# A two-layer decoder trunk on one core: in layer 1's channel mixer the last plain chunk of columns moves to the front, and the last grouped one ends the mixer with its columns turned one token tile at a time

## The chip, the core and the metric

The kernel runs on one core of a Trainium2 chip. The engines that matter here are TensorE (PE in the profile; PEld is its weight load), VectorE (DVE), ScalarE (ACT), GpSimd (POOL) and SyncE (SP), which issues most DMA loads. Each engine works through its own queue in order and waits on semaphores for the others. The metric is the device time of one launch in microseconds (us), lower is better; before the change it is 571.77 us, the median of three runs (570.83 to 571.89).

## What is computed

256 tokens of width 1024 go through two layers. Each layer is a token mixer beside a small cross-attention, an output projection and a LayerNorm, and then the channel mixer, which is all that the change touches:

```python
def swiglu(x, w_in, w_out):
    g, u = jnp.split(x @ w_in, 2, axis=-1)
    return (jax.nn.silu(g) * u) @ w_out

x = layer_norm(ALPHA * x + swiglu(x, w_ffn_in[i], w_ffn_out[i]), ln_ffn_g[i], ln_ffn_b[i])
```

`w_in` is 1024 x 5632 and `w_out` 2816 x 1024, all in float32.

## The kernel before

**Split numbers.** Every matmul operand is written as a high and a low part: ACT rounds a value to the multiplier's format (`split`, L234) and DVE subtracts that from the original (L235). A product takes three matmuls (high x high, high x low, low x high). So each weight passes over ACT and over DVE before TensorE can use it. `Stream` does this in *halves*: a 1 MB unit of weights is loaded into one of four raw buffers and split in two halves of 128 x 1024 into one of ten split buffers (`HALF_BUFS`). The order of the halves is that of `ffn_steps`, so the table in that function sets the loads, the splits and the matmuls alike. TensorE's order is that of the code; the other engines' order is set by a scheduler at build time.

**Chunks.** The 2816 columns are eleven chunks of 256. A *plain* chunk ("R", `chunk_in`) multiplies the 256 tokens (two token tiles of 128, written tt 0 and 1) by the chunk's gate and value columns in four steps (i = 0 to 3) of one half each. A *grouped* pair of chunks ("S", `product`) gets by with seven products instead of eight, by sums of quarters (in Strassen's way): M1, M5, M2, M3, M6, M7, M4, two halves each. The left sums are made once a layer (`sums`, tiles `Sg`). The weight sums are made by DVE on the raw operands: an add of 128 x 2048 (L189) ahead of M5, M6 and M4; for M7 a load that accumulates does it (L192). Operands "11" and "21" have one buffer each for all groups (tags `gb` and `vbig`); `gb` also takes the final LayerNorm's scale and shift (`gb1ffn`). PSUM tiles X, Y and Z take the products. After some products DVE combines them: m1 += Y (L605), u2 += Z (L609), m1 = -m1*u2 (L610), m5 += X (L612, after M7 and before M4 overwrites X), m5 = -m5*silu (L616).

**Out.** A chunk's activations are turned by four transposes (`transposes`, L625; tile `tp`, split into `htg`), and `chunk_out` multiplies them by two halves of `w_out` ("out" steps, `spl_w`) into the accumulators `fog`. Each "out" step for both token tiles is twelve matmuls of 128 x 512, as long as one product or one step of a plain chunk.

**Order of layer 1 before.** R0 and R1 (with tile 0's steps first, since tile 1's input comes later), then S2, S4, S6, S8, then R10. The out steps of earlier chunks stand between the products. At the end `end_tile(0)` finishes tile 0 with chunks 9 and 10 and its LayerNorm starts; `last_tile(1)` runs chunks 8 to 10 of tile 1 in three column pieces, each followed by its part of the last LayerNorm, and the results are stored.

Of the kernel before, what the change touches and what calls it, by code (L numbers as in the profile page):

```python
# [21 lines left out]
P = 128  # L22
# [13 lines left out]
NFF = D_FF // 256  # L36
# [3 lines left out]

PLAN = (("R", 0), ("R", 1), ("S", 2), ("S", 4), ("S", 6), ("S", 8), ("R", 10))
PRODUCTS = ("M1", "M5", "M2", "M3", "M6", "M7", "M4")

OPERAND = {"M1": ("11", None), "M5": ("11", "12"), "M2": ("21", None), "M3": ("22", None),
# [4 lines left out]
def ffn_steps(l):  # L51

    steps, due, prev = [], [], []
    for kind, c in PLAN:
        new = [("out", p, k, (0, 1)) for p in prev for k in range(2)]
        if kind == "S":


            ins = [("s", c, m) for m in PRODUCTS]
            due += new  # L60
            early, due = due[:-3], due[-3:]
            steps += [ins[0], ("tp",), *early[:1], ins[1], *early[1:], *ins[2:5], due[0], ins[5], due[1], ins[6]]
            due = due[2:]
        else:
            ins = [("r", c, i, (0, 1)) for i in range(4)]
            if l == 1 and c == 0:

                steps += [*(("r", 0, i, (0,)) for i in range(4)), *(("r", 1, i, (0,)) for i in range(2)), ("x",)]
            elif l == 1 and c == 1:
                steps += [*(("r", 1, i, (0,)) for i in range(2, 4)), *(("r", 0, i, (1,)) for i in range(4)),  # L70
                          *(("r", 1, i, (1,)) for i in range(2)), ("tp",), *(("r", 1, i, (1,)) for i in range(2, 4))]
                due = new
            elif c == NFF - 1:
                steps += [ins[0], ("tp",), *due, *ins[1:], *(("out", NFF - 3, k, (0,)) for k in range(2)), ("tp",)]
            elif c:
                steps += [ins[0], ("tp",), *ins[1:]]
                due = new
            else:
                steps += ins
        prev = [c, c + 1] if kind == "S" else [c]  # L80
    return steps
# [140 lines left out]
def build(nc, tc, ins, out):  # L222
    ET = mybir.EngineType
    with (
# [44 lines left out]
        for i in range(WARM):  # L269
            nc.tensor.matmul(wt[:, :P], warm, warm, start=True, stop=True)  # L270
        ident = const.tile([P, P], F32, name="ident")
# [6 lines left out]
            out=maskb, in_=maskb, compare_op=ALU.is_ge, fill=NEG, base=0,  # L278
# [248 lines left out]
        class Ffn:  # L527
# [52 lines left out]
            def product(self, c, m):  # L580


                if m == "M1":
                    self.X, self.Y, self.Z = (mm_tile(f"{n}{self.nm}{c}") for n in "XYZ")
                dst = {"M1": self.X, "M6": self.X, "M7": self.X, "M4": self.X, "M2": self.Y}.get(m, self.Z)
                alone = m in ("M1", "M5", "M2")
                for x in range(2):
                    w = stream.get(f"s{self.l}_{c}", m, x)
                    for k in range(2):
                        for n, (a, b) in enumerate(PASSES):  # L590
                            mm(dst, self.left[m](a, 2 * x + k), w[:, b, k * 512:(k + 1) * 512],
                               alone and x == 0 and k == 0 and n == 0, x == 1 and k == 1 and n == 2, not alone)
                    stream.done(f"s{self.l}_{c}", m, x)

                def kept(n, src):
                    t = work_tile(f"{n}{self.nm}{c}")
                    nc.scalar.copy(t, src)
                    return t

                if m == "M1":  # L600
                    self.m1 = kept("m1", self.X)
                elif m == "M5":
                    self.m5 = kept("m5", self.Z)
                elif m == "M2":
                    nc.vector.tensor_add(self.m1, self.m1, self.Y)  # L605
                    nc.scalar.activation(self.m1, self.m1, AF.Silu)
                elif m == "M6":
                    u2 = kept("u2", self.X)
                    nc.vector.tensor_add(u2, u2, self.Z)  # L609
                    nc.vector.scalar_tensor_tensor(self.m1, self.m1, -1.0, u2, ALU.mult, ALU.mult)  # L610
                elif m == "M7":
                    nc.vector.tensor_add(self.m5, self.m5, self.X)  # L612
                elif m == "M4":
                    sg = work_tile(f"sg{self.nm}{c}")
                    nc.scalar.activation(sg, self.X, AF.Silu)
                    nc.vector.scalar_tensor_tensor(self.m5, self.m5, -1.0, sg, ALU.mult, ALU.mult)  # L616
                    self.pending.append([(c + j, [h[:, 256 * j:256 * j + 256] for h in (self.m1, self.m5)])
                                         for j in range(2)])

            def transposes(self):  # L620

# [13 lines left out]
            def run(self, mid=None):  # L635
                for st in ffn_steps(self.l):
                    self.tp_tiles()
                    if st[0] == "r":
                        self.chunk_in(*st[1:])
                        if st[1:3] == (NFF - 1, 0):  # L640
                            stream.held = {"gb", "vbig"}
                            self.gb = load_gb(self.l, "ffn")
                    elif st[0] == "s":
                        self.product(*st[1:])
                    elif st[0] == "x":
                        mid()
                    elif st[0] == "tp":
                        if self.pending:
                            self.transposes()
                    else:  # L650
                        self.chunk_out(*st[1:])
                return self.gb
# [57 lines left out]
        for i in range(4):  # L710
# [11 lines left out]
            out=wsT, in_=wsT, compare_op=ALU.is_ge, fill=0.0, base=0,  # L722
# [9 lines left out]
        for h in range(2):  # L732
            for tt in range(2):
                sl = slice(h * 384, (h + 1) * 384)
# [9 lines left out]
        for j in range(4):  # L744
            t = actp.tile([P, 2, 512], F32R, tag="hm", name=f"memT{j}", bufs=4)
# [39 lines left out]
        gb = load_gb(0, "mix")  # L785
# [16 lines left out]
        ffn = Ffn(0, x_of(x1T), xres, "f")  # L802
        stream.held.clear()
        ffn.sums(A)
        gb = ffn.run()
# [72 lines left out]
        for i in range(6):  # L878
# [16 lines left out]
            if i == 2:  # L895
                gb = load_gb(1, "mix")
# [29 lines left out]
            ffn.sums(A)  # L926

        gb = ffn.run(second_tile)
        ffn.end_tile(0).finish(gb, store=True)
        ffn.last_tile(1).finish(gb, store=True)  # L930


# [5 lines left out]
def _pack(inp):  # L938
    a, b = inp["a_w_in"][0], inp["b_w_in"][0]
    kv, wo, fi, fo = inp["w_mem_kv"], inp["w_mix_out"], inp["w_ffn_in"], inp["w_ffn_out"]  # L940
    blk = {}
    for i in range(4):
        blk[f"v{i}"] = _cols(a, 2 * i, 2 * i + 2, W_MIX, 2 * W_MIX)
        blk[f"bv{i}"] = _cols(b, 2 * i, 2 * i + 2, 2 * W_MIX, 3 * W_MIX)
    blk["qm0"] = _cols(a, 0, KT, 2 * W_MIX, 2 * W_MIX + W_MEM)
    blk["qm1"] = _cols(b, 0, KT, 3 * W_MIX, 3 * W_MIX + W_MEM)
    for i in range(3):
        blk[f"u{i}"] = _cols(a, 0, KT, 256 * i, 256 * i + 256)
    for l in range(2):
        blk[f"km{l}"] = _cols(kv[l], 0, KT, 0, W_MEM)  # L950
        blk[f"vm{l}"] = _cols(kv[l], 0, KT, W_MEM, 2 * W_MEM)
        for i in range(4):
            blk[f"o{l}_{i}"] = _cols(wo[l], 2 * i, 2 * i + 2, 0, D)
        for kind, c in PLAN:
            g, v = fi[l][:, 256 * c:], fi[l][:, D_FF + 256 * c:]
            for h in range(2):
                rows = KT // 2 * h, KT // 2 * (h + 1)
                if kind == "S":
                    blk[f"s{l}_{c}_{h + 1}1"], blk[f"s{l}_{c}_{h + 1}2"] = (_cols(m, *rows, 0, 512) for m in (g, v))
                else:  # L960
                    blk[f"r{l}_{c}_{'AB'[h]}"] = _cols(np.concatenate([g[:, :256], v[:, :256]], axis=1), *rows, 0, 512)
        for c in range(NFF):
            blk[f"w{l}_{c}"] = _cols(fo[l], 2 * c, 2 * c + 2, 0, D)
    for i in range(6):
        q = b[:, 128 * i:128 * i + 128]
        k = b[:, W_MIX + 128 * i:W_MIX + 128 * i + 128]
        blk[f"qk{i}"] = _cols(np.concatenate([q, k], axis=1), 0, KT, 0, 256)
    flat = np.concatenate([blk[n].reshape(-1) for n, _ in weight_units()])
    return {
        "w": flat,  # L970
        "x": np.ascontiguousarray(inp["x"][0]),
        "xT": np.ascontiguousarray(inp["x"][0].T),
        "memT": np.ascontiguousarray(inp["mem"][0].T),
        "wsT": np.ascontiguousarray(inp["a_w_s"][0].transpose(2, 0, 1)),
        "bs": np.ascontiguousarray(inp["a_b_s"][0].reshape(6, 2, P).transpose(1, 0, 2)),
        "a_ln_v_g": inp["a_ln_v_g"], "a_ln_v_b": inp["a_ln_v_b"],
        "ln_mix_g": inp["ln_mix_g"], "ln_mix_b": inp["ln_mix_b"],
        "ln_ffn_g": inp["ln_ffn_g"], "ln_ffn_b": inp["ln_ffn_b"],
    }
# [19 lines left out]
```

## Time and profile before

| what | value |
|---|---|
| timed runs, median (lowest, highest) | 571.77 us (570.83, 571.89) |
| profiled execution, its own time | 571.07 us |
| its span, first to last instruction | 569.4 us |
| PE busy | 554.5 us, 97% |
| DVE busy | 499.4 us, 88% |
| ACT busy | 358.5 us, 63% |
| layer 1's channel mixer, TensorE | from 381.2 us (first `pg`) to 561.4 us (last matmul) |

Times in the rows are microseconds from the start of the span, durations in ns where marked. A row of a timeline may merge several instructions of one kind (x12); then its second figure is from the first one's start to the last one's end. Instructions on PE, DVE and ACT overlap a little, so the distance from start to start is somewhat less than the duration.

### The profile page before, as it was taken

How to read it: one execution, taken by the hardware profiler on the slowest of the kernel's cores; microseconds unless marked ns; L12 is line 12 of the kernel's file. 1: busy time of each engine (PE TensorE's matmuls, PEld its weight loads, DVE VectorE, ACT ScalarE, POOL GpSimd, SP SyncE). 2: the span in 40 equal slices, each digit the busy share in tenths (PEclk: the TensorE clock that was granted, in tenths of full speed). 3: DMA queues.
4: the chain of work that ended last, by engine and by line, in shares of the span. 5: the costliest groups of instructions: out<-in, count | busy, mean ns of one | idle time of the engine just before them, and what ended most of it. 6: DMA issues, size and time to landing. Idle time of an engine off the chain costs nothing.

```text
span 569.4 us, 8025 instructions
## 1 busy us (share of the span) xinstructions
PE 554.5 (97%) x3064; PEld 478.1 (84%) x3064; DVE 499.4 (88%) x639; ACT 358.5 (63%) x550; POOL 22.1 (4%) x32
## 2 busy tenths in 40 slices
PE   8999999999999999999999999999999999999994
PEld 7999879888888888888999998788878787887884
DVE  5797989999998999995987897497999999999936
ACT  6766957677665747862377979465575747569500
POOL 2020000000000000000000000000000000000001
PEclk9999999999999999999999999999999999999997
DMA  8996686447776385685576232434358395757402
GB/s 295 394 362 268 236 329 229 172 97 303 193 280 199 112 325 124 277 312 218 200 286 254 76 120 104 147 148 148 75 220 281 131 337 138 302 143 281 162 1 74
DMA packets 21335, 118.88 MB, mean 209 GB/s; under 512 B 2352, under 2 KB 5552, under 8 KB 8880
## 3 DMA queue, kind: packets, MB, share of 16 engines
q1 hardware_dynamic: 19856, 109.72, 51.7%
q0 software_dynamic: 1152, 8.39, 7.9%
q8 instruction: 24, 0.39, 0.3%
q10 hardware_dynamic: 288, 0.26, 0.1%
q14 instruction: 15, 0.12, 0.1%
HBM read 117.31 MB, written 1.05 MB: 208 GB/s over the span
## 4 chain that ended last, share of the span: by engine, by line
PE 86%; DVE 9%; ACT 2%; issue 1%; DMA 1%; SPq 0%; POOLq 0%; ACTq 0%
PE fof L258 11%; PE fog L258 9%; PE Xf L258 8%; PE Xg L258 7%; PE pf L258 6%; PE opc L258 4%; PE opa L258 4%; PE Zf L258 4%; PE qk L258 4%; PE pg L258 3%; PE pu L258 3%; PE bv L258 3%; PE pvm L258 3%; PE va L258 3%; DVE raw_s L189 2%; DVE spl_s_M L235 2%
## 5 line engine op out<-in xcount | busy, mean ns | idle before, releaser
L234 ACT CAST spl_s_M<-raw_s 128x1024 fp32r<-128x1024 f32 x112 | 114.2, 1052 | 44.7 <-DVE raw_s L189 35.3
L235 DVE TENSOR_TENSOR spl_s_M<-raw_s,spl_s_M 128x1024 fp32r<-128x1024 f32 x112 | 132.1, 1219 | 4.9 <-ACT spl_s_M L234 4.6
L258 PE MATMUL fof<-spl_w,htf 128*128 128x512 f32 x264 | 63.8, 392 | 0.0
L258 PEld LDWEIGHTS fof<-spl_w,htf 128*128 128x128 f32 x264 | 49.0, 188 | 10.0
L258 PE MATMUL fog<-spl_w,htg 128*128 128x512 f32 x228 | 55.3, 392 | 0.0
L189 DVE TENSOR_TENSOR raw_s<-raw_s,raw_s 128x2048 f32<-128x2048 f32 x24 | 54.9, 2285 | 0.1
L235 DVE TENSOR_TENSOR spl_w<-raw_w,spl_w 128x1024 fp32r<-128x1024 f32 x44 | 52.9, 1218 | 0.0
L258 PEld LDWEIGHTS fog<-spl_w,htg 128*128 128x128 f32 x228 | 42.4, 188 | 8.6
L234 ACT CAST spl_w<-raw_w 128x1024 fp32r<-128x1024 f32 x44 | 45.5, 1050 | 4.3 <-DVE spl_w L235 2.3
L258 PE MATMUL qk<-x2T,spl_qk 128*128 128x256 f32 x288 | 36.7, 285 | 0.0
L258 PEld LDWEIGHTS qk<-x2T,spl_qk 128*128 128x128 f32 x288 | 35.2, 192 | 0.0
L258 PE MATMUL Xg<-spl_s_M,SgM 128*128 128x512 f32 x96 | 24.3, 395 | 3.9 <-DVE spl_s_M L235 3.9
L258 PEld LDWEIGHTS Xg<-spl_s_M,SgM 128*128 128x128 f32 x96 | 17.7, 188 | 9.2 <-DVE spl_s_M L235 5.6
L258 PE MATMUL opc<-spl_o,mix 128*128 128x512 f32 x96 | 23.5, 397 | 0.0
L258 PE MATMUL Xf<-spl_s_M,SfM 128*128 128x512 f32 x96 | 23.1, 389 | 0.0
L258 PE MATMUL Zf<-spl_s_M,SfM 128*128 128x512 f32 x96 | 23.1, 389 | 0.0
L258 PE MATMUL Zg<-spl_s_M,SgM 128*128 128x512 f32 x96 | 23.1, 389 | 0.0
L258 PE MATMUL Xg<-spl_s_M,x3T 128*128 128x512 f32 x96 | 22.6, 389 | 0.0
L258 PE MATMUL Xf<-spl_s_M,x1T 128*128 128x512 f32 x96 | 22.6, 389 | 0.0
L258 PE MATMUL opa<-spl_o,mix 128*128 128x512 f32 x96 | 22.5, 392 | 0.0
L258 PEld LDWEIGHTS Xf<-spl_s_M,SfM 128*128 128x128 f32 x96 | 18.0, 188 | 3.8
L258 PEld LDWEIGHTS Xf<-spl_s_M,x1T 128*128 128x128 f32 x96 | 18.0, 188 | 3.7
(236 smaller groups left out, 1099.9 us busy)
## 6 DMA issues: line engine op xcount, KB each, us to landing
raw_s<-in_w SPq DMA_DIRECT2D x32, 1024.0 KB, 4.9
raw_w<-in_w SPq DMA_DIRECT2D x22, 1024.0 KB, 5.5
raw_o<-in_w SPq DMA_DIRECT2D x8, 1024.0 KB, 6.1
raw_s<-in_w POOLq DMA_DIRECT2D x8, 1024.0 KB, 7.9
raw_r_A<-in_w SPq DMA_DIRECT2D x6, 1024.0 KB, 4.8
raw_r_B<-in_w SPq DMA_DIRECT2D x6, 1024.0 KB, 4.9
raw_qk<-in_w SPq DMA_DIRECT2D x6, 1024.0 KB, 4.9
raw_u<-in_w SPq DMA_DIRECT2D x3, 1024.0 KB, 9.6
```

The source lines that it names most:

```text
L189: self.nc.vector.tensor_add(self.raw[parts[0]], self.raw[parts[0]], self.raw[parts[1]])
L234: nc.scalar.copy(hi, src)
L235: nc.vector.tensor_sub(lo, src, hi.bitcast(F32))
L258: nc.tensor.matmul(o, lhsT, rhs, start=start, stop=stop, skip_group_check=on)
```

## The change

The table `PLAN` becomes one per layer; layer 0 keeps its own. In layer 1 the plain chunk of the end stands third: R0, R1, R2, S3, S5, S7, S9. So the groups take the chunk pairs 3-4, 5-6, 7-8 and 9-10. The out steps of the plain chunks pile up and are all done in the first group (`due += new`). In the last group the out steps of chunk 8 are done for token tile 0 alone. Since m1 holds token tile 0 and m5 token tile 1 of a group's result, and m1 is complete after M6 while m5 needs M4, the new `turn_tile` transposes tile 0 of chunks 9 and 10 ahead of M4 and tile 1 after it, within `end_tile(0)`. The load of the final scale and shift stands behind M4 of the last group instead of the first step of R10.

```diff
-PLAN = (("R", 0), ("R", 1), ("S", 2), ("S", 4), ("S", 6), ("S", 8), ("R", 10))
+PLANS = ((("R", 0), ("R", 1), ("S", 2), ("S", 4), ("S", 6), ("S", 8), ("R", 10)),
+         (("R", 0), ("R", 1), ("R", 2), ("S", 3), ("S", 5), ("S", 7), ("S", 9)))
...
             early, due = due[:-3], due[-3:]
+            if c == NFF - 2:
+
+                steps += [ins[0], ("tp",), *early, *ins[1:5], due[0], ins[5], ("out", c - 1, 0, (0,)), ("turn", c, 0),
+                          ("out", c - 1, 1, (0,)), ins[6]]
+                continue
...
-                due = new
+                due += new
...
-                    self.pending.append([(c + j, [h[:, 256 * j:256 * j + 256] for h in (self.m1, self.m5)])
-                                         for j in range(2)])
+                    if c < NFF - 2:
+                        self.pending.append([(c + j, [h[:, 256 * j:256 * j + 256] for h in (self.m1, self.m5)])
+                                             for j in range(2)])
+
+            def turn_tile(self, c, tt):
+
+                if tt == 0:
+                    self.turn.append([mm_tile(f"tp{self.nm}{c + j}").rearrange("p (k t) -> p k t", k=2) for j in range(2)])
+                sl = slice(tt * P, (tt + 1) * P)
+                for j, tp in enumerate(self.turn[0]):
+                    h = (self.m1, self.m5)[tt][:, 256 * j:256 * j + 256]
+                    for k in range(2):
+                        nc.tensor.transpose(tp[:, k, sl], h[:, k * P:(k + 1) * P], ident)
+                    ht = self.ht_tile(c + j)
+                    split(ht[:, 0, :, sl], ht[:, 1, :, sl], tp[:, :, sl])
...
+                        if st[1:] == (NFF - 2, "M4"):
+                            self.gb = load_gb(self.l, "ffn")
+                    elif st[0] == "turn":
+                        self.turn_tile(*st[1:])
...
-        ffn.end_tile(0).finish(gb, store=True)
+        ffn.end_tile(0, lambda: ffn.turn_tile(NFF - 2, 1)).finish(gb, store=True)
```

The built programs show what this moves. Line numbers of the changed kernel are 6 higher from the table on, and more behind `turn_tile`. First, TensorE between the last step of chunk 1 and the first out step, before: `pg` is a plain chunk's tile, `Xg` the tile of M1, `tpg` the transposes, `fog` an out step.

```order
L258 MATMUL pg_3946<-spl_r_1_B_3904,x3T 128x512 x6
L258 MATMUL Xg_3981<-spl_s_2_M_0_3984,x3T 128x512 x6
L258 MATMUL Xg_3981<-spl_s_2_M_1_3993,x3T 128x512 x6
L625 MATMUL tpg_3980<-ident,hg_3915 128x128 x4
L258 MATMUL fog_4011<-spl_w_0_0_4015,htg_3963 128x512
```

And the same place of the changed kernel:

```order
L264 MATMUL pg_3944<-spl_r_1_B_3902,x3T 128x512 x6
L264 MATMUL pg_3982<-spl_r_2_A_3979,x3T 128x512 x6
L264 MATMUL pg_3989<-spl_r_2_A_3979,x3T 128x512 x6
L644 MATMUL tpg_3978<-ident,hg_3913 128x128 x4
L264 MATMUL pg_3982<-spl_r_2_A_4003,x3T 128x512 x6
L264 MATMUL pg_3989<-spl_r_2_A_4003,x3T 128x512 x6
L264 MATMUL pg_3982<-spl_r_2_B_4022,x3T 128x512 x6
L264 MATMUL pg_3989<-spl_r_2_B_4022,x3T 128x512 x6
L264 MATMUL pg_3982<-spl_r_2_B_4037,x3T 128x512 x6
L264 MATMUL pg_3989<-spl_r_2_B_4037,x3T 128x512 x6
L264 MATMUL Xg_4060<-spl_s_3_M_0_4063,x3T 128x512 x6
```

The four steps of chunk 2 (48 matmuls) now stand between chunk 1 and the first group; the four transposes of chunk 1 move into them.

Second, DVE from the end of one group's splits to the next group's first ones, before (group 4 to group 6, with buffer numbers, since the rows would read alike):

```order
L235 TENSOR_TENSOR spl_s1_4_M7_1_4372<-raw_s1_4_12_4177,spl_s1_4_M7_1_4372 128x1024
L609 TENSOR_TENSOR u2g4_4344<-u2g4_4344,Zg4_4198 128x512
L235 TENSOR_TENSOR spl_w1_3_0_4382<-raw_w1_3_4236,spl_w1_3_0_4382 128x1024
L610 SCALAR_TENSOR_TENSOR m1g4_4217<-m1g4_4217,u2g4_4344 128x512
L235 TENSOR_TENSOR spl_s1_4_M4_0_4398<-raw_s1_4_21_4181,spl_s1_4_M4_0_4398 128x1024
L235 TENSOR_TENSOR spl_s1_4_M4_1_4407<-raw_s1_4_21_4181,spl_s1_4_M4_1_4407 128x1024
L612 TENSOR_TENSOR m5g4_4270<-m5g4_4270,Xg4_4196 128x512
L235 TENSOR_TENSOR spl_s1_6_M1_0_4434<-raw_s1_6_11_4410,spl_s1_6_M1_0_4434 128x1024
```

The changed kernel, group 5 to group 7:

```order
L195 TENSOR_TENSOR raw_s1_5_21_4292<-raw_s1_5_21_4292,raw_s1_5_11_4286 128x2048
L241 TENSOR_TENSOR spl_w1_4_0_4493<-raw_w1_4_4347,spl_w1_4_0_4493 128x1024
L611 TENSOR_TENSOR m1g5_4328<-m1g5_4328,Yg5_4308 128x512
L241 TENSOR_TENSOR spl_s1_5_M4_0_4509<-raw_s1_5_21_4292,spl_s1_5_M4_0_4509 128x1024
L241 TENSOR_TENSOR spl_s1_5_M4_1_4518<-raw_s1_5_21_4292,spl_s1_5_M4_1_4518 128x1024
L615 TENSOR_TENSOR u2g5_4455<-u2g5_4455,Zg5_4309 128x512
L616 SCALAR_TENSOR_TENSOR m1g5_4328<-m1g5_4328,u2g5_4455 128x512
L241 TENSOR_TENSOR spl_s1_7_M1_0_4545<-raw_s1_7_11_4521,spl_s1_7_M1_0_4545 128x1024
L241 TENSOR_TENSOR spl_s1_7_M1_1_4554<-raw_s1_7_11_4521,spl_s1_7_M1_1_4554 128x1024
L241 TENSOR_TENSOR spl_w1_4_1_4579<-raw_w1_4_4347,spl_w1_4_1_4579 128x1024
L195 TENSOR_TENSOR raw_s1_7_11_4521<-raw_s1_7_11_4521,raw_s1_7_12_4523 128x2048
L618 TENSOR_TENSOR m5g5_4381<-m5g5_4381,Xg5_4307 128x512
```

The combination of m5 with X (L612 before, L618 now) stood ahead of the next group's splits and now stands behind three of them and an add of raw operands. The add for M4 (first row), which in every group of before stands ahead of the splits for M6, stands behind them in groups 3 and 5 and ahead of them again in groups 7 and 9.

Third, DVE at the end of the mixer, before (r1_10 is the last plain chunk, fog10 and fog11 are tile 1's accumulators):

```order
L235 TENSOR_TENSOR spl_w1_9_0_5026<-raw_w1_9_4934,spl_w1_9_0_5026 128x1024
L235 TENSOR_TENSOR spl_w1_9_1_5035<-raw_w1_9_4934,spl_w1_9_1_5035 128x1024
L235 TENSOR_TENSOR spl_w1_10_0_5045<-raw_w1_10_4951,spl_w1_10_0_5045 128x1024
L235 TENSOR_TENSOR spl_w1_10_1_5051<-raw_w1_10_4951,spl_w1_10_1_5051 128x1024
L687 SCALAR_TENSOR_TENSOR xres_868<-xres_868,fog10_4013 128x512
```

And in the changed kernel:

```order
L241 TENSOR_TENSOR spl_s1_9_M4_1_5007<-raw_s1_9_21_4762,spl_s1_9_M4_1_5007 128x1024
L618 TENSOR_TENSOR m5g9_4866<-m5g9_4866,Xg9_4777 128x512
L241 TENSOR_TENSOR spl_w1_9_0_5022<-raw_w1_9_4932,spl_w1_9_0_5022 128x1024
L241 TENSOR_TENSOR htg9_4980<-tpg9_4976,htg9_4980 128x2x128
L241 TENSOR_TENSOR htg10_4985<-tpg10_4977,htg10_4985 128x2x128
L241 TENSOR_TENSOR spl_w1_9_1_5031<-raw_w1_9_4932,spl_w1_9_1_5031 128x1024
L241 TENSOR_TENSOR spl_w1_10_0_5049<-raw_w1_10_4958,spl_w1_10_0_5049 128x1024
L241 TENSOR_TENSOR spl_w1_10_1_5055<-raw_w1_10_4958,spl_w1_10_1_5055 128x1024
L622 SCALAR_TENSOR_TENSOR m5g9_4866<-m5g9_4866,sgg9_5016 128x512
```

The last four splits of `w_out` come directly behind the last group's splits, and m5's last product, for which the transposes of tile 1 wait, stands behind them.

## Rows read from the trace of the kernel before

**Rows 1.** The page: busy time, share of the span and instructions; chain by engine.
```profile
PE 554.5 (97%) x3064; PEld 478.1 (84%) x3064; DVE 499.4 (88%) x639; ACT 358.5 (63%) x550; POOL 22.1 (4%) x32
...
PE 86%; DVE 9%; ACT 2%; issue 1%; DMA 1%; SPq 0%; POOLq 0%; ACTq 0%
```

**Rows 2.** Waits of PE from 355 to 570 us: total, times, longest.
```profile
PE Xg L258 <- DVE spl_s_M L235: 3.9, 4, 1.2
```

**Rows 3.** Timeline of PE: start, length, what, idle before it and releaser.
```profile
389.38 1.04 PE L359 MATMUL ptc<-ident,xres 128*128 128x128 f32 x8
...
398.46 2.89 PE L258 MATMUL pg<-spl_r_A,x3T 128*128 128x512 f32 x12
401.19 0.60 PE L625 MATMUL tpg<-ident,hg 128*128 128x128 f32 x4
...
404.39 2.88 PE L258 MATMUL Xg<-spl_s_M,x3T 128*128 128x512 f32 x12
...
419.27 2.83 PE L258 MATMUL Xg<-spl_s_M,SgM 128*128 128x512 f32 x11 [0.42 <-DVE spl_s_M L235]
...
451.60 2.79 PE L258 MATMUL Xg<-spl_s_M,SgM 128*128 128x512 f32 x11 [1.18 <-DVE spl_s_M L235]
```

**Rows 4.** Stretches: two whole groups, then the end of the mixer.
```profile
435.55:467.83 32.28, 31.11 (x142) 25.52 (x141) 31.51 (x28) 21.10 (x26) 0.82 (x2) 1.00 0.68 225
467.83:500.14 32.31, 31.14 (x141) 25.53 (x140) 31.52 (x28) 21.13 (x26) 0.78 (x2) 1.00 0.68 228
...
532.43:552.88 20.45, 20.45 (x97) 17.04 (x96) 11.97 (x16) 6.22 (x9) 0.00 (x0) 1.00 0.12 48
```

**Rows 5.** Timeline of DVE ahead of the second group's M6.
```profile
440.56 4.63 DVE L235 TENSOR_TENSOR spl_s_M<-raw_s,spl_s_M 128x1024 fp32r<-128x1024 f32 x4
445.10 2.28 DVE L189 TENSOR_TENSOR raw_s<-raw_s,raw_s 128x2048 f32<-128x2048 f32 x1
447.51 0.69 DVE L605 TENSOR_TENSOR m1g<-m1g,Yg 128x512 f32<-128x512 f32 x1
448.12 2.29 DVE L189 TENSOR_TENSOR raw_s<-raw_s,raw_s 128x2048 f32<-128x2048 f32 x1
450.32 2.35 DVE L235 TENSOR_TENSOR spl_s_M<-raw_s,spl_s_M 128x1024 fp32r<-128x1024 f32 x2
```

**Rows 6.** Timeline of DVE ahead of the first group.
```profile
386.29 1.41 DVE L351 SCALAR_TENSOR_TENSOR xres<-xres,rsc,gb1mix 128x512 f32<-128x512 f32 x2
387.62 0.41 DVE L576 TENSOR_TENSOR hg<-hg,pg 128x256 f32<-128x256 f32 x1
390.64 1.29 DVE L235 TENSOR_TENSOR x3T<-ptc,x3T 128x512 fp32r<-128x512 f32 x2 [2.60 <-ACT x3T L234]
392.58 0.69 DVE L544 TENSOR_TENSOR Ac<-Ac,Ac 128x512 f32<-128x512 f32 x1 [0.65 <-ACT Ac L365]
...
397.98 1.22 DVE L235 TENSOR_TENSOR spl_s_M<-raw_s,spl_s_M 128x1024 fp32r<-128x1024 f32 x1
```

**Rows 7.** Groups of instructions from 404 to 536 us, on ACT, by shape.
```profile
L234 ACT CAST spl_s_M<-raw_s 128x1024 fp32r<-128x1024 f32 x54 | 55.1, 1052 | 22.1 <-DVE raw_s L189 17.8 <-DMA raw_s<-in_w 4.2
...
L615 ACT ACTIVATE sgg<-Xg 128x512 f32<-128x512 f32 x4 | 2.4, 595 | 14.3 <-PE Xg L258 14.3
...
L597 ACT COPY u2g<-Xg 128x512 f32<-128x512 f32 x4 | 2.3, 574 | 0.0
```

**Rows 8.** DMA issues from 505 to 545 us: count, KB each, us to landing.
```profile
raw_w<-in_w SPq DMA_DIRECT2D x3, 1024.0 KB, 6.1
...
gb1ffn<-in_ln_ffn_b SPq DMA_DIRECT2D x1, 512.0 KB, 8.3
```

**Rows 9.** Chain that ended last, its end: start, length, what.
```profile
553.04 8.40 PE last L258 x54
...
561.47 0.43 DVE xres L694
```

More of the change, by code (lines that the diff above doesn't have):

```diff
@@ L53, in ffn_steps @@
     steps, due, prev = [], [], []
-    for kind, c in PLAN:
+    for kind, c in PLANS[l]:
         new = [("out", p, k, (0, 1)) for p in prev for k in range(2)]
@@ L76, in ffn_steps @@
                 steps += [ins[0], ("tp",), *ins[1:]]
-                due = new
+                due += new
             else:
@@ L953, in _pack @@
             blk[f"o{l}_{i}"] = _cols(wo[l], 2 * i, 2 * i + 2, 0, D)
-        for kind, c in PLAN:
+        for kind, c in PLANS[l]:
             g, v = fi[l][:, 256 * c:], fi[l][:, D_FF + 256 * c:]
```

## The prediction

> **What bounds the kernel now.** I read the page first. TensorE is busy 97% of the span and holds 86% of the chain that ended last [rows 1], so the time is TensorE's work plus the gaps in it, plus what follows its last matmul. The change removes no matmul and no transpose: the four steps of one plain chunk stand elsewhere, and the eight transposes of the last group come as four and four. So only gaps can move.
>
> The waits of PE in layer 1 are one row: four waits for DVE's splits of weights, 3.9 us together [rows 2]. PE's timeline shows each behind the first matmul of an M6, 0.42 us in the first group and 1.18 in the second [rows 3]; the third and fourth have the same row with 1.17. That is 0.42 + 1.18 + 1.17 + 1.17 = 3.94 us.
>
> Why at M6: the stretches of two whole groups last 32.3 us each, PE is busy 31.1 and DVE 31.5 of it [rows 4], and DVE's timeline ahead of M6 has no gap worth the name between its rows [rows 5]. So DVE sets the pace inside the groups and loses some 1.2 us on PE in each. Behind the groups it is the other way round: in the last 20.5 us DVE is busy 12.0 while PE is full [rows 4]. That slack stands where nothing is left to make. The reader is to see a producer that is too slow in the middle and idle at the end.
>
> **Prices, start to start.** A split of one half costs DVE 1.14 us (four in 4.63, the last of 1.22), an add of raw operands 2.20 (448.12 to 450.32), a 128x512 operation 0.61 (447.51 to 448.12) [rows 5]. A step, product or out step costs PE 2.72 (398.46 to 401.19) [rows 3]. I call margin the time from a half being split to its first use.
>
> **The change part by part.**
> *Chunk 2 ahead of the groups.* Its four steps put 4 x 2.72 = 10.9 us of PE work before the first M1. Two of its four splits fall into gaps that DVE has ahead of x3T and of the sums (2.60 and 0.65 us, [rows 6]). The first of these stands inside the LayerNorm of tile 1 and delays its end from 387.7 (386.29 + 1.41, [rows 6]) to 388.8; PE's transposes that read it begin at 389.38 [rows 3], so it is hidden with 0.55 us to spare, and each us beyond that would cost PE one. The other two splits delay M1's by 2.3. Before, M1's first half was ready at 397.98 + 1.22 = 399.2 [rows 6] and used at 404.39 [rows 3], a margin of 5.2. Now it is ready at 401.5 and used at 415.3: 13.8, a gain of 8.6.
>
> *Margin at the first M6.* Before it was -0.42. Two more out steps come between M1 and M6 (5.4 us of PE). DVE has two more splits for them (2.3) and chunk 2's activations (two 128x256 products, estimated at 0.33 each from the 0.41 of [rows 6], and one 0.61), but M4's add (2.2) stands behind M6 there. So -0.42 + 8.6 + 5.4 - 1.3 = 12.3. The ten split buffers allow more: the half ten places earlier is the second of M1, free at 418.0, which with ACT's 1.05 [rows 7] and DVE's 1.22 gives 420.3 for a use at 434.8, so up to 14.5.
>
> *Following groups.* Group 5 has the same rows between its M6 and group 3's: 12.3 - 1.2 = 11.1. There the lead is cut, since DVE's order puts u2's combination, which waits for M6, behind the splits of M4. From the end of M6 on DVE needs ACT's copy 0.57 [rows 7], u2 and m1 1.2, three splits 3.4, an add 2.2 and m5 += X 0.7, together 8.1 us. PE has three steps, 8.2, before M4 overwrites X. That is an added wait, with M4 and all of PE queued behind it; with semaphores I bound it by 0 and 0.6 and take 0.3, the middle, as the two sums are nearly equal. M5's first half of group 7 is then ready 9.2 after the end of M6 and used 17.2 after it (three steps, M4, M1, eight transposes of some 0.1, an out step): margin 8.0. To group 7's M6 DVE has seven splits, three small operations and both adds (14.2) against four steps (10.9): 4.7 left. Group 9 costs another 1.2: 3.5. ACT waited 4.2 us for loads in the three later groups of before, 1.4 each [rows 7]; if the last two groups lose that too, 0.7 is left. All four M6 waits go.
>
> *The end.* From group 9's M6 to the second half of M4, DVE has eight splits and three small operations (10.9), PE 12.7: the margin grows by 1.8 to 5.3. From there to m5's last product, for which the transposes of tile 1 wait, DVE has four splits, m5 += X, two narrow splits (0.33 each) and the product (6.5), PE half a product and chunk 9's out step for tile 0 and both halves (4.1): 2.9 left, or 0.1 in the poor case. That product also needs the silu after M4: 0.60 on ACT [rows 7] and 0.69 on DVE, less than the 2.72 of PE work before the transposes. If this cover is gone it costs PE what is missing, one for one. The scale and shift are issued behind M4's add, ahead of the last M6; the slowest such load takes 8.3 us [rows 8], and their use is over 20 us away. The four narrow splits that replace two cost DVE and ACT 0.1 each in all, inside the margins.
>
> *After the last matmul* nothing differs: the 54 matmuls of tile 1's pieces and the LayerNorm behind them are the same rows [rows 9].
>
> Sum: -3.94 + 0.3 = -3.6. The profiled execution took 571.07 us (span 569.4): 567.5. The timed runs, 570.83 to 571.89, have a mean of 571.50, 0.43 above it, so I forecast 567.9 for the timed median.
>
> **The rivals.**
> *Half of it.* The lead is built but loads come too late to keep it: operands 11 and 21 have one buffer each, and when DVE is early it waits for the landing, 6.1 us for a 1 MB unit in [rows 8]. Then the waits of M6 in groups 7 and 9 stay (2.3) and 0.3 is added: -1.3, or 570.2. For it: ACT already waits 1.4 a group for such loads. Against it: the margins stay positive after that loss.
>
> *No change.* The gaps are a matter of buffers, not of the order, and come back elsewhere: 571.1 to 571.8. Against it: DVE is at work in the rows ahead of M6 and isn't held by a buffer [rows 5].
> The Trainium skill (Perfetto Trace Analysis, Optimization Strategy) says that the same gap repeating on the engine that should be saturated can mean too little SBUF or PSUM for the next tile. By that rule more buffers, not another order, would close these gaps, and the time would stay. The trace doesn't bear it out: all four gaps of [rows 2] end with DVE's split.
>
> *Slower.* One mechanism: in group 5, m5 += X stands behind M4's splits, the next M1's, an out split and an add, and PE's M4 waits for it. From M6's first split DVE needs ten splits, two adds and four small operations to get there, 18.2 us; PE gets there in four steps, 10.9. So with a margin m at that M6, PE waits 7.3 - m. My m is 11.1. At 3.4 the gain of 3.94 is eaten; at m = 1 it is 6.3 - 3.94 = +2.4: 573.5, or 573.9 timed; with m = 0 and the first two M6 waits also kept (1.6), +5. For it: the order really has these rows, and the scheduler put them there. Against it: m would have to lose 8 us out of 11.
>
> **How the numbers follow.** All or nearly all waits gone 0.78; half of it 0.08; no change 0.07; slower 0.07. What a measurement of this kernel can tell from no change is about 0.2%, 1.1 us. The half case lies on the fast side of that bound by a hair, so I give it half to each: faster 0.83, within 0.2% 0.10, slower 0.07. The range runs from the full 3.94 off the fastest run, 566.8, to the half case, 570.3; the likeliest case by itself is 567.1 to 568.6.
>
> **What would show it right or wrong.** Right: no PE wait at any M6 of layer 1, the first M1 of the groups near 415.3, DVE idle ahead of u2 in group 5, at most 0.6 us of wait before that group's M4, PE gapless through the transposes of tile 1, and 8.4 us of PE work in the last pieces as before. Wrong: a wait of PE at M4 in group 5 for DVE above 1 us; M6 waits left in groups 7 and 9; a wait before tile 1's transposes; DVE idle for loads between groups; or a later start of the transposes at 389.38. The forecast falls if DVE reaches group 5's M6 with less than 7 us in hand.

## The result

The changed kernel takes 567.07 us (median of four runs, 566.84 to 567.38) against 571.83 us before in the same runs: ratio 0.9921 (of the means), 95% interval 0.9904 to 0.9938. Measured again beside the experiments it was 566.88 against 571.40, 0.9921 (0.9909 to 0.9933). It is 0.8% faster; 567.9 had been forecast, in a range of 566.8 to 570.3.

The profiled execution took 567.08 us (span 565.4), 3.99 us less than that of before. PE is 98% busy, and its waits between 355 and 570 us are down from [rows 2] to this row (columns: us in total, times, longest):

```profile
PE Xg L264 <- DVE m5g L618: 0.3, 1, 0.3
```

The four waits at M6 are gone and one new wait stands where the prediction put it, at the M4 of group 5. PE's timeline of the changed kernel (start, length, what, idle before it):

```profile
381.62 1.75 PE L264 MATMUL pg<-spl_r_A,x3T 128*128 128x512 f32 x7
...
389.79 1.04 PE L365 MATMUL ptc<-ident,xres 128*128 128x128 f32 x8
...
416.21 2.89 PE L264 MATMUL Xg<-spl_s_M,x3T 128*128 128x512 f32 x12
...
435.73 2.88 PE L264 MATMUL Xg<-spl_s_M,SgM 128*128 128x512 f32 x12
...
466.58 2.88 PE L264 MATMUL Xg<-spl_s_M,SgM 128*128 128x512 f32 x12
...
474.74 2.88 PE L264 MATMUL fog<-spl_w,htg 128*128 128x512 f32 x12
477.95 5.74 PE L264 MATMUL Xg<-spl_s_M,x3T 128*128 128x512 f32 x24 [0.33 <-DVE m5g L618]
...
498.02 2.88 PE L264 MATMUL Xg<-spl_s_M,SgM 128*128 128x512 f32 x12
...
528.87 2.88 PE L264 MATMUL Xg<-spl_s_M,SgM 128*128 128x512 f32 x12
...
545.68 0.60 PE L635 MATMUL tpg<-ident,m5g 128*128 128x128 f32 x4
546.04 3.00 PE L264 MATMUL fog<-spl_w,htg 128*128 128x512 f32 x12
548.87 0.39 PE L264 MATMUL last<-spl_w,htg 128*128 128x512 f32 x1
```

To be seen here: the four M6 (435.73, 466.58, 498.02, 528.87) run as twelve matmuls without a break, where [rows 3] has one matmul, a wait and eleven. The first M1 comes at 416.21, and tile 1's transposes (545.68) follow their out step without a gap. For the length of the stretch and the price of a wait, four rows of PE's timeline of the kernel before:

```profile
381.21 1.52 PE L258 MATMUL pg<-spl_r_A,x3T 128*128 128x512 f32 x6
...
418.47 0.39 PE L258 MATMUL Xg<-spl_s_M,SgM 128*128 128x512 f32 x1
...
450.03 0.39 PE L258 MATMUL Xg<-spl_s_M,SgM 128*128 128x512 f32 x1
...
552.88 8.55 PE L258 MATMUL last<-spl_w,htg 128*128 128x512 f32 x54
```

From the first plain step to the last pieces it took 552.88 - 381.21 = 171.67 us and takes 548.87 - 381.62 = 167.25 now: 4.42 less. (That the mixer starts 0.41 later in this execution is no effect of the change: over all profiled executions its start lies between 380.99 and 382.31.)

DVE's timeline shows where the margins come from; the first row ends tile 1's LayerNorm, then M1, M6 of groups 3 and 5, u2 and m5 of group 5, M6 of groups 7 and 9, and m5's last product:

```profile
387.67 1.41 DVE L357 SCALAR_TENSOR_TENSOR xres<-xres,rsc,gb1mix 128x512 f32<-128x512 f32 x2
...
400.96 2.35 DVE L241 TENSOR_TENSOR spl_s_M<-raw_s,spl_s_M 128x1024 fp32r<-128x1024 f32 x2
...
421.71 1.22 DVE L241 TENSOR_TENSOR spl_s_M<-raw_s,spl_s_M 128x1024 fp32r<-128x1024 f32 x1
...
455.59 2.35 DVE L241 TENSOR_TENSOR spl_s_M<-raw_s,spl_s_M 128x1024 fp32r<-128x1024 f32 x2
...
470.12 0.69 DVE L615 TENSOR_TENSOR u2g<-u2g,Zg 128x512 f32<-128x512 f32 x1 [2.49 <-ACT u2g L603]
...
477.22 0.68 DVE L618 TENSOR_TENSOR m5g<-m5g,Xg 128x512 f32<-128x512 f32 x1
...
492.85 2.36 DVE L241 TENSOR_TENSOR spl_s_M<-raw_s,spl_s_M 128x1024 fp32r<-128x1024 f32 x2
...
525.49 1.22 DVE L241 TENSOR_TENSOR spl_s_M<-raw_s,spl_s_M 128x1024 fp32r<-128x1024 f32 x1
...
543.79 0.69 DVE L622 SCALAR_TENSOR_TENSOR m5g<-m5g,sgg 128x512 f32<-128x512 f32 x1 [0.40 <-ACT sgg L621]
```

| margin, from the end of the first split to its first use | forecast, us | measured, us |
|---|---|---|
| LayerNorm of tile 1 to its transposes | 0.55 | 389.79 - 389.08 = 0.71 |
| first M1 | 13.8 | 416.21 - 402.18 = 14.0 |
| M6 of group 3 | 12.3 | 435.73 - 422.93 = 12.8 |
| M6 of group 5 | 11.1 | 466.58 - 456.81 = 9.8 |
| M6 of group 7 | 4.7 | 498.02 - 494.07 = 4.0 |
| M6 of group 9 | 3.5 (0.7 with waits for loads) | 528.87 - 526.71 = 2.2 |
| m5's last product to tile 1's transposes | 2.9 (0.1) | 545.68 - 544.48 = 1.2 |

### The profile page after: what moved, and what is told of

It reads as the page before. It is cut to its first block, busy times and chain, and to the rows that moved or that the text cites. A ratio compares the mean times of both kernels' runs of the same rounds, so it can differ in the third digit from the quotient of the medians.

```text
span 565.4 us, 8050 instructions
## 1 busy us (share of the span) xinstructions
PE 554.6 (98%) x3064; PEld 479.4 (85%) x3064; DVE 499.3 (88%) x641; ACT 360.6 (64%) x552; POOL 22.5 (4%) x32
## 3 DMA queue, kind: packets, MB, share of 16 engines
HBM read 117.31 MB, written 1.05 MB: 209 GB/s over the span
## 4 chain that ended last, share of the span: by engine, by line
PE 85%; DVE 8%; ACT 2%; DMA 2%; issue 2%; SPq 0%; POOLq 0%; ACTq 0%; DVEq 0%
PE fof L264 11%; PE Xf L264 8%; PE fog L264 6%; PE pf L264 6%; PE pg L264 6%; PE Xg L264 5%; PE opc L264 4%; PE opa L264 4%; PE Zf L264 4%; PE qk L264 4%; PE pu L264 3%; PE bv L264 3%; PE pvm L264 3%; PE Zg L264 3%; PE va L264 3%; PE hkm L264 2%
## 5 line engine op out<-in xcount | busy, mean ns | idle before, releaser
L264 PE MATMUL Xg<-spl_s_M,SgM 128*128 128x512 f32 x96 | 23.1, 389 | 0.0
L264 PEld LDWEIGHTS Xg<-spl_s_M,x3T 128*128 128x128 f32 x96 | 17.9, 188 | 4.5 <-DVE m5g L618 0.8
```

The lines of the kernel that those rows point to most:

```text
L264: nc.tensor.matmul(o, lhsT, rhs, start=start, stop=stop, skip_group_check=on)
```

## The experiments

Four theories were set against each other. *Lead*: DVE is too slow inside the groups and idle in plain chunks; with the plain chunk ahead, it is in front by the groups' deficit before they begin. *End*: only what happens at the mixer's end counts. *Buffers*: the repeating gaps come from too few buffers. *Order*: the gain comes from the scheduler's having put M4's add behind M6 in two groups. Every kernel was timed against the kernel before on its own chip, which took 571.18 us beside r4_third, r6_fourth, whole_turn and x_first, 571.12 beside the three b_ kernels and 571.40 beside the last three rows. The times in the expectations start from 571.5 to 571.8, so the ratios and stretches decide, not the times alone. "Waits shown" is the idle column of PE's timeline; "stretch" is taken from PE's timeline as above, and an undisturbed stretch is about 166.5 us (b_noadd).

| kernel | median, us | ratio of means to before (95%) | PE waits shown, us | stretch, us |
|---|---|---|---|---|
| before | 571.83 | | 3.9 in four M6 | 171.67 |
| changed | 567.07 | 0.9921 (0.9904 to 0.9938) | 0.3 at M4 | 167.25 |
| r4_third | 566.53 | 0.9920 (0.9908 to 0.9933) | 0.4 in one M6 | 167.60 |
| r6_fourth | 567.91 | 0.9946 (0.9933 to 0.9958) | 1.6 in two M6 | 168.79 |
| whole_turn | 568.49 | 0.9956 (0.9943 to 0.9968) | 1.5 in three places | 169.02 |
| x_first | 566.92 | 0.9923 (0.9909 to 0.9936) | none over 0.15 | 167.39 |
| b_noadd | 566.22 | 0.9911 (0.9898 to 0.9925) | none | 166.51 |
| b_bufs8 | 571.12 | 1.0002 (0.9993 to 1.0011) | 4.0 in four M6 | 171.65 |
| b_m4late | 582.82 | 1.0200 (1.0186 to 1.0214) | 8.9 in thirteen places | 183.69 |
| changed_again | 566.88 | 0.9921 (0.9909 to 0.9933) | 0.2 at M4 | 167.09 |
| x_before_w | 566.88 | 0.9925 (0.9912 to 0.9939) | none | 166.71 |
| r4_x | 566.63 | 0.9918 (0.9904 to 0.9931) | 0.4 in one M6 | 167.43 |

**The plain chunk one and two groups later** (r4_third, r6_fourth), the end as changed:

```diff
-         (("R", 0), ("R", 1), ("R", 2), ("S", 3), ("S", 5), ("S", 7), ("S", 9)))
+         (("R", 0), ("R", 1), ("S", 2), ("R", 4), ("S", 5), ("S", 7), ("S", 9)))
...
+         (("R", 0), ("R", 1), ("S", 2), ("S", 4), ("R", 6), ("S", 7), ("S", 9)))
```

> The changed kernel with the plain chunk of layer 1 one group later: R0, R1, S2, R4, S5, S7, S9; the end as changed. Lead theory (VectorE gets ahead of TensorE while a plain chunk runs, and each group eats about 1.4 us of that, counted start to start): the M6 wait of the first group stays (0.4 us shown, 0.7 start to start), those of the second to fourth are gone; 3.9 to 4.4 us faster than before, so 567.1 to 567.9. End theory (only the plain chunk's leaving the end and the turning by token tiles count): no M6 wait anywhere in layer 1, the same time as the changed kernel or less, 566.5 to 567.1.

> The changed kernel with the plain chunk of layer 1 after two groups: R0, R1, S2, S4, R6, S7, S9; the end as changed. Lead theory: the M6 waits of the first two groups stay (0.4 and 1.2 shown, 0.7 and 1.4 start to start), none in S7 and S9; 2.5 to 3.1 us faster than before, so 568.4 to 569.3. End theory: as the changed kernel, 566.5 to 567.3. No gain at all (571.8) would say that the lead has to be built before the first group.

PE's waits of the first, then of the second:

```profile
PE Xg L264 <- DVE spl_s_M L241: 0.4, 1, 0.4
```
```profile
PE Xg L264 <- DVE spl_s_M L241: 1.6, 2, 1.2
```

Each group that runs ahead of the plain chunk keeps its wait, with the size it had before (0.42; 0.42 + 1.18), and each behind it has none. Both ends are the changed one, so the end alone doesn't make the gain; the place of the slack does. By time r4_third can't be told from the changed kernel, since its one M6 wait is about as long as the wait at M4 that it lacks; r6_fourth is slower (567.87 to 568.35 in its five runs, 566.50 to 566.77 in those of r4_third beside it), as the lead theory has it. Both medians missed the lead theory's ranges, 0.6 and 0.5 us below them, and r4_third's 566.53 lies in the end theory's. Part of that is the kernel before, 0.65 us quicker here than 571.83; another part is that both kernels take 16.07 us behind the last pieces' start, where the kernel before and the changed one take 16.5, and why stays open. So against the end theory stand the waits that stayed and the time of r6_fourth, not the time of r4_third.

**The columns turned whole** (whole_turn): the chunk moved, the other half of the change undone.

```diff
-                steps += [ins[0], ("tp",), *early, *ins[1:5], due[0], ins[5], ("out", c - 1, 0, (0,)), ("turn", c, 0),
-                          ("out", c - 1, 1, (0,)), ins[6]]
+                steps += [ins[0], ("tp",), *early, *ins[1:5], due[0], *ins[5:], ("out", c - 1, 0, (0,)),
+                          ("out", c - 1, 1, (0,)), ("tp",)]
...
-        ffn.end_tile(0, lambda: ffn.turn_tile(NFF - 2, 1)).finish(gb, store=True)
+        ffn.end_tile(0).finish(gb, store=True)
```

> The changed kernel with the chunk moved to the front, but the last group's columns turned whole: M4, both half out steps of chunk 8 for token tile 0, then all eight transposes, then the end. Lead theory: the M6 waits are gone as in the changed kernel; at the end TensorE waits for the split of the turned columns between the transposes and the first matmul of chunk 9, ScalarE 0.6 and VectorE 0.7, so 1.3 us, and perhaps one more us before M4, since two half steps no longer stand ahead of it: 1.3 to 2.5 us slower than the changed kernel, 568.4 to 569.6, still faster than before. End theory (the gain is that of the turning): no faster than before, 571 to 572.

PE's timeline at the end of this kernel (M4 of group 9, then chunk 9's out step behind the transposes):

```profile
538.88 3.02 PE L264 MATMUL Xg<-spl_s_M,x3T 128*128 128x512 f32 x12 [1.05 <-DVE m5g L618]
...
545.74 5.76 PE L264 MATMUL fog<-spl_w,htg 128*128 128x512 f32 x24 [0.24 <-ACT htg L240]
```

The total was as expected, 1.8 us of stretch more than the changed kernel and still faster than before, but it stands elsewhere: most of it is M4's wait for m5 += X, which the two half out steps and the turn of tile 0 cover in the changed kernel. Behind the transposes PE lost only 0.24 shown, since its first matmul needs ACT's high part alone. So the turning by tiles is worth 1.8 of the 4.4 us; without it the move alone gains some 2.6.

**The wait at group 5's M4** (x_first: m5 += X ahead of the next raw add; x_before_w: ahead of one out split only; r4_x: the first with the chunk order of r4_third). Each adds an ordering edge on DVE, and r4_x moves the chunk besides; the edge of x_first and r4_x:

```diff
-            self.nc.vector.tensor_add(self.raw[parts[0]], self.raw[parts[0]], self.raw[parts[1]])
+            add = self.nc.vector.tensor_add(self.raw[parts[0]], self.raw[parts[0]], self.raw[parts[1]])
+            if key[1] == "M5" and key[0][:2] == "s1" and self.x_read:
+                self.behind(add, self.x_read)
```

> The changed kernel with one order fixed in layer 1: the combination of m5 with X stands ahead of the next group's raw add for M5 on VectorE. If the 0.33 us wait (0.6 start to start) before group 5's M4 is the queue on VectorE, it is gone. Lead theory: the 2.2 us add now comes later for its own readers, and the margin there (about 8 us in group 7) hides it: 566.3 to 567.1, 0.0 to 0.6 us faster than the changed kernel, which a measurement hardly tells. Rival: the margin is thinner than thought and the wait turns up at group 7's transposes or at group 9's M6 instead: the same time or up to 0.6 us slower.

> The changed kernel with one order fixed in layer 1: only the second out split of chunk 4 stands behind the combination of m5 with X on VectorE, one split (1.1 us) less ahead of it. The wait before group 5's M4 (0.3 shown, 0.5 to 0.6 start to start) goes and nothing else is late, since the out split has some 8 us of margin: the stretch falls from 167.2 to 166.6 to 166.9 us, 0.3 to 0.6 us less, at the edge of what a measurement can tell. Rival, as with the raw add put behind it: the wait turns up later in the groups, and the stretch stays at 167.2 to 167.5.

> The plain chunk one group later (R0, R1, S2, R4, S5, S7, S9) with the combination of m5 with X ahead of the next raw add. The first group's M6 wait stays (0.4 shown, 0.7 start to start); the 0.24 before a group's transposes goes: stretch 167.1 to 167.5, the same time as the changed kernel within 0.3 us.

> The changed kernel itself, on the same chip and beside the same runs of the kernel before as the other two of this call: 4.4 us of TensorE's waits less than before, ratio 0.991 to 0.993, 566.4 to 567.2. Its stretch from the first plain step to the last pieces 167.2 us, of which 0.6 at group 5's M4.

In x_first and x_before_w the wait at M4 is gone, so it is DVE's queue that holds it. In x_first two smaller delays turn up instead, at the transposes of group 3's columns (0.15 us) and at group 9's M6 (its second matmul comes 0.31 us late), and the stretch is no shorter: the rival of its expectation. x_before_w has the shortest stretch of the kernels that leave nothing out, 166.71, within its forecast; the changed kernel, run again beside it, has 167.09 with 0.17 us shown at M4. In r4_x the first group's M6 wait stays, as set, and its stretch lies in its range. But by time neither it nor r4_x can be told from the changed kernel (the intervals overlap, medians within 0.3 us of each other). No version was found that measurably beats it.

**VectorE's work made less** (b_noadd), in the kernel before:

```diff
-        if len(parts) == 2 and key[-1] == 0:
+        if len(parts) == 2 and key[-1] == 0 and not (key[1] == "M4" and key[0][:2] == "s1"):
```

> The kernel before, with the raw add ahead of M4 left out in all four groups of layer 1 (2.2 us of VectorE each; M4 then uses operand 21 alone, so its result is another). TensorE's matmuls and the order of chunks are those of before. If VectorE's work per group (32.3 us against TensorE's 31.1) makes the waits, taking 2.2 us off makes it 30.1: all four M6 waits go and the time falls by 4.4 to 5.0 us to 566.8 to 567.4, without any chunk being moved. Buffer theory (too few buffers make the repeating gaps): the waits stay, 571.8.

No wait is left, without any chunk moved, and the time falls by 4.9 us or 0.9%, as the pace of DVE asks for (the median itself lies 0.6 us below its range, since the kernel before took 571.12 here). Without the add the next load of operand 11 can start earlier too, and ACT's waits for loads of operands between 400 and 530 us are down from 4.2 to 0.2 us; but those waits don't explain the gaps, since in the kernel before DVE's rows had no idle behind them.

**Fewer buffers** (b_bufs8): `HALF_BUFS = 8` instead of 10 in the kernel before.

> The kernel before with eight split buffers instead of ten, in both layers. Pace theory (VectorE is simply too slow inside the groups): the four M6 waits of layer 1 stay as they are, 3.9 us shown; at most 0.3 us more elsewhere: 571.5 to 572.1. Buffer theory (the repeating gaps come from too few buffers): with fewer the gaps grow, by a half's 1.1 us of VectorE work or more in each of the four groups, 576 or more.

```profile
PE Xg L258 <- DVE spl_s_M L235: 4.0, 4, 1.2
```

The same four waits and the same time within 0.1% (571.12 us, as the kernel before beside it, and thus below the 571.5 set for it): the buffer theory, that of the prediction's second rival, falls for the split buffers. The raw buffers and PSUM were not varied by themselves; against them speaks that b_noadd and the changed kernel lose the M6 waits with every buffer count as it was.

**The order of M4's add alone** (b_m4late): the kernel before, with an edge that puts that add behind the splits of M6.

```diff
+            if key[1] == "M4" and key[0][:2] == "s1":
+                self.behind(add, self.last_m6)
```

> The kernel before with one order fixed in layer 1: the raw add for M4 stands behind the splits of M6 on VectorE, as the scheduler has it in groups 3 and 5 of the changed kernel. Order theory (the gain comes from that place of the add): the M6 waits go, up to 4 us faster. Lead theory: work per group is the same 32.3 us, so a wait of about 1.4 per group turns up somewhere else: not faster than 571. Since the add is also the last reader of operand 11, whose one buffer takes the next group's operand, the next group's load starts later, by up to the two splits and an out split or more, and M1 can wait for it: up to 3 us per group slower, 572 to 581.

PE's waits:

```profile
PE Xg L267 <- DVE spl_s_M L239: 4.5, 9, 0.8
PE Xg L267 <- ACT spl_s_M L238: 4.0, 3, 1.6
PE Zg L267 <- DVE spl_s_M L239: 0.4, 1, 0.4
```

2% slower. The order theory falls: without a lead the late add only moves the waits, most of all to the next group's M1, because the add is the last reader of operand 11 and the next group's load into that one buffer starts later (the three waits on ACT's split; ahead of the first of them ACT had itself waited 2.93 us for the landing). So the early add ahead of M6 in the kernel before was no mistake of the scheduler's. The 1.8 us above the upper end of the expectation (581) were not foreseen; part of what lies beyond the waits is TensorE's clock (last section).

The chunk experiments speak against the order theory more directly. In r4_third the adds stand ahead of M6 in every group, as in the kernel before, and the groups behind the plain chunk have no M6 wait all the same. DVE's two adds and the splits of M6 in its group 5, then that M6 on PE:

```profile
453.68 4.61 DVE L195 TENSOR_TENSOR raw_s<-raw_s,raw_s 128x2048 f32<-128x2048 f32 x2
458.21 2.36 DVE L241 TENSOR_TENSOR spl_s_M<-raw_s,spl_s_M 128x1024 fp32r<-128x1024 f32 x2
```
```profile
466.74 2.88 PE L264 MATMUL Xg<-spl_s_M,SgM 128*128 128x512 f32 x12
```

## Why the prediction was right

**Which term.** "Only gaps can move" held: matmuls and transposes cost the same, the stretch changed by its gaps, and behind the last piece the times agree (16.47 and 16.50 us from its first matmul to the span's end).

**The lead.** The working of margins held in sign at all seven places of the table above; in size it held to 0.5 us in the first three and was 0.7 to 1.7 us too large in the last four. From group 3's M6 to group 5's 3.0 us were lost where 1.2 had been set, with no term for the difference. DVE's and ACT's timelines of the changed kernel behind M6's first split of group 3 show it:

```profile
422.85 2.29 DVE L195 TENSOR_TENSOR raw_s<-raw_s,raw_s 128x2048 f32<-128x2048 f32 x1
425.05 1.22 DVE L241 TENSOR_TENSOR spl_s_M<-raw_s,spl_s_M 128x1024 fp32r<-128x1024 f32 x1
...
428.92 1.23 DVE L241 TENSOR_TENSOR spl_s_M<-raw_s,spl_s_M 128x1024 fp32r<-128x1024 f32 x1 [0.38 <-ACT spl_s_M L240]
431.62 1.23 DVE L241 TENSOR_TENSOR spl_w<-raw_w,spl_w 128x1024 fp32r<-128x1024 f32 x1 [1.48 <-ACT spl_w L240]
```
```profile
427.83 1.06 ACT L240 CAST spl_s_M<-raw_s 128x1024 fp32r<-128x1024 f32 x1 [1.24 <-PE fog L264]
...
430.54 1.05 ACT L240 CAST spl_w<-raw_w 128x1024 fp32r<-128x1024 f32 x1 [1.65 <-PE fog L264]
```

DVE is idle for 0.38 + 1.48 = 1.9 us behind ACT's splits, and these wait for the end of an out step on PE, which used the half ten places earlier: the lead had reached the ten split buffers. The prediction reckoned that limit at group 3's M6 (14.5) and not behind it. (The rows also show that in group 3 M4's add stands between the two splits of M6, not behind both; only in group 5 is it behind both.) Groups 7 and 9 came out 0.7 and 1.3 lower than the sum without loads, inside the bound given for group 9. In the table's last row the 1.2 us are set by the silu, for which the product waits 0.40 us, and not by DVE's queue: they are to be held against 2.72 - 0.60 - 0.69 = 1.4 of the prediction's other term. At the front, both hidden splits came out of the 2.60 us ahead of x3T, where 0.50 are left; the 0.65 ahead of the sums stayed.

**The added wait.** It stands where it was put, and for the reason given: DVE waits for M6 at u2 (2.49 us idle in the row at 470.12), and from there its queue ends at 477.90, PE's three steps at 477.46. Forecast 0.3, shown 0.33. That it was met so nearly is luck: the two sums were equal within 0.1, the 0.3 was the middle of a bound of 0 to 0.6, and start to start the wait cost 0.60.

**What was mis-sized.** The price of a wait. "-3.94 + 0.3 = -3.6" took the idle column, and the stretch fell by 4.42. In the first wait the matmul behind it starts 419.27 - 418.47 = 0.80 us after the one ahead of it ([rows 3] and the rows above), where undisturbed ones are 0.23 apart, so 0.57 is lost where 0.42 is shown; the idle counts only from the modelled end of a matmul that takes 0.39 but lets the next one start after 0.23. The next start is 0.11 late as well. Counted so, the four waits cost 0.69 + 3 x 1.44 = 5.0 us and the new one 0.60: 4.4, the whole difference. The forecast of 567.9 is 0.8 too high for that reason; the median, 567.07, lies at the lower edge of the likeliest case (567.1 to 568.6), for which the prediction gives no working. The ends of the range are each 0.1 us wider than their own sums (570.83 - 3.94 = 566.9 and 571.5 - 1.3 = 570.2), which changes nothing here.

**The rivals.** Half of it: no M6 wait stayed. No change: the time contradicts it, and b_bufs8 its mechanism. Slower: the mechanism is real (whole_turn shows the same queue holding M4 for 1.05 us in group 9), but with 9.8 us in hand at group 5's M6, where 7.3 were needed, DVE had 2.5 to spare and spent them idle ahead of u2; the 0.6 lost at that M4 come from the rows behind u2.

## What to carry to other kernels

When a producer is slower than its consumer in one kind of stage and idle in another, the stages' order matters: put the one with slack first, as far as buffers hold the lead (here ten split buffers capped it in the first group), and work out the lead at each later use, not only at the first. Price a wait of TensorE from start to start, not by the idle column: here each cost 0.27 us more than was shown. Before a repeating gap is put down to buffers, look whether the producer is at work in the rows ahead of it.

## What was not expected of the hardware

In b_m4late TensorE's clock gave way for some 3 us behind the longer waits. Two stretches of 2 us, at the second late M1 and behind it (columns: stretch and its length; PE, PEld, DVE, ACT, POOL busy; granted clock; DMA share; GB/s):

```profile
472.00:474.00 2.00, 2.00 (x6) 1.52 (x6) 2.00 (x3) 0.00 (x0) 0.00 (x0) 0.50 0.00 0
...
476.00:478.00 2.00, 2.00 (x12) 1.70 (x11) 1.29 (x2) 2.00 (x5) 0.84 (x1) 1.00 1.11 360
```

The granted clock was 0.50 between 472 and 474 us, the lower of the two levels (1.2 GHz), and the matmuls there start 0.43 us apart instead of 0.23. Ahead of it PE had waited 0.52, 1.62 and 0.77 us between 465.0 and 471.2 us. The same happened at the next group's M1 at 508 to 512. Some eight matmuls, 0.2 us late each, twice over, make about 3.2 us. In the kernel before, with single waits of at most 1.2 us, 32 us apart, the granted clock stayed at 1.00 [rows 4]. No run here separates what of those waits brought the clock down.
